# Splitting the gated outputs of an RWKV-7 layer in the rounds that make them, and loading the split halves at the output projection

## The chip, the cores and the metric

The kernel runs on one core of a Trainium2 chip. The metric is the device time of one execution in microseconds (us). Names of engines as in the profile: PE is TensorE (matmuls), PEld its weight loads, DVE is VectorE, ACT is ScalarE, POOL is GpSimd, SP is SyncE, which here only issues DMAs. A q behind a name (SPq) is the engine's instruction queue.

## The reference, cut to what matters

Two residual layers over 512 tokens of width 2048. Layer 0 is gated differential attention; the change is in layer 1, RWKV-7 time mixing:

```python
for i in range(DEPTH):                       # DEPTH = 2
    hn = rms_norm(x, norm_w[i])
    ...
    x = x + out

def rwkv7_mixer(h, ...):
    p = h @ w_in                             # r, k, v, gate g and two low-rank parts
    p = p + (token_shift(p) - p) * mu
    ...
    y = wkv7_scan(rh, decay, kh, vh, -kk, kk * ah)   # 32 heads of 64, a state of 64x64 per head
    ...                                      # group norm over each head, bonus term
    y = y.reshape(B, T, RW_WIDTH) * jax.nn.silu(g)   # the gated output, 512 x 2048
    return y @ w_out, v_first                # the output projection, 2048 x 2048
```

## The kernel before

**Split products.** Every large product of float32 matrices is made of three fp32r matmuls: each operand is split into a high part (hi, a copy rounded to fp32r) and a low part (lo, operand minus hi), and hi·hi, hi·lo and lo·hi are added up in PSUM. `split_w` splits a weight block: it is loaded to `wraw` (512 KB, SP issues the load at L78), ACT copies the high part to `wh` (L105), DVE subtracts the low part to `wl` (L106). The tokens that weights are multiplied with stand in two pools of 16 places each, `hH` and `hL`, one place per 128 channels ("row" k: 128 x 512).

**Layer 1** runs in 16 rounds j, one pair of heads (128 channels) each. `proj(i, j)` projects the layer's tokens to r, k, v or gate (48 matmuls, L125). The scan of the pair before is cut into steps that a `Chain` puts between those matmuls: matmuls `sm` (L1654, L1665, L1672) and `Y` on PE, copies `rhs` and `VS` on ACT (L1657, L1667), `VS` on DVE (L1676), `SA` and `Sg` on POOL (L1660, L1663). Each round solves a small triangular system `Tm` on DVE (L1516, L1518, behind POOL's memset at L1507); it goes to DRAM (`td`, L1526), comes back in four small loads `TT<-td` on SP (L1545), and DVE transposes it (`T`, L1555) for 32 small matmuls `px` (L1561), from which the next scan starts. The output of a pair is group-normed and multiplied by its gate (`mixv`, made by `shift_mix` on ACT at L1283 and DVE at L1284, weighted at L1620). `gated` does the last product on DVE (L1627) and has POOL store the row to `yd2` in DRAM (L1628).

**Output projection.** When the tokens of the layer are no longer used (during the projections of the last two gates), `split_rows` loads the rows of 14 pairs from `yd2`, in the order 8 to 13, then 0 to 7, to work tiles `yr` (SP, L462), and splits each to a place of `hH` (ACT, L452) and `hL` (DVE, L453). The last two rows are split straight from SBUF later. `seven_early` then computes output columns 0 to 1023. It begins with plain products of rows 8 to 13 and the first weight blocks, which `loader` fetches to three buffers `wraw`, while the last pair's scan still runs between them; then come seven Strassen products ("11", "12", "S1" and so on), whose summed rows (`frow`, L687, L699, L700) are formed from `yd2` as well. `between(n)` puts the end of the last two pairs between these pieces. `seven` computes columns 1024 to 2047. `acc` (L1875) are the residual's blocks.

The Tile scheduler sets the order of each engine's instructions and DMA issues by program order and priority (`high_priority(offset)` moves instructions ahead; `AHEAD` is 2000); every engine works its row off in order, and so does each queue. Tiles of one tag share buffers, so a load to a tag waits for the last reader of the buffer.

Of the kernel before, what the change touches and what calls it, by code (L numbers as in the profile page):

```python
# [13 lines left out]
F32 = mybir.dt.float32  # L14
F32R = mybir.dt.float32r
# [8 lines left out]
P = 128  # L24
D = 2048
T = 512
# [12 lines left out]
AHEAD, SCAN, SOLVE = 2000, 3000, 4000  # L39
# [34 lines left out]
def load_w(g, raw, part, k0, ks, queue=None):  # L74

    w, c = part
    with g.tc.issue_after(g.last) if g.last and not queue else ExitStack():
        ld = (queue or g.nc.sync).dma_start(out=raw[:, ks.start : ks.stop], in_=w[c][:, k0 + ks.start : k0 + ks.stop])  # L78
    g.last = ld.ins if g.last and not queue else g.last
    return ld.ins  # L80
# [367 lines left out]
def split_row(g, yr):  # L448
    nc = g.nc
    hh = g.hp.tile([P, T], F32R, name="hH", tag="hH")  # L450
    hl = g.hp.tile([P, T], F32R, name="hL", tag="hL")
    nc.scalar.copy(hh[:], yr)  # L452
    g.rowsplit = nc.vector.tensor_sub(hl[:], yr, hh[:].bitcast(F32)).ins  # L453
    return hh, hl


def split_rows(g, src, tags, bufs, order):

    out = {}
    for i, k in enumerate(order):  # L460
        yr = g.work.tile([P, T], F32, name="yr", tag=tags[i % len(tags)], bufs=bufs)
        g.nc.sync.dma_start(out=yr[:], in_=src[k * P : (k + 1) * P, :])  # L462
        out[k] = split_row(g, yr[:])
    return [out[k] for k in sorted(out)]


NH4 = 8
KG = 2
# [417 lines left out]
    done("21")  # L886


def loader(g, w, homes):

    homes = list(homes)

    def load(k0, c):
        homes.append(homes.pop(0))
        pool, tag, bufs = homes[-1]
        raw = pool.tile([P, KG, 512], F32, name="wraw", tag=tag, bufs=bufs)
        g.fetched = load_w(g, raw, (w, c), k0, slice(0, KG))
        return raw

    return load  # L900


def flat(t):

    n = "abc"[: len(t.shape) - 1]
    n = " ".join(n)
    return t[:].rearrange(f"p {n} -> p ({n})").rearrange("p (k c) -> p k c", k=KG)


def layer0(g, aps):  # L910
    nc, tc = g.nc, g.tc
    with ExitStack() as cx:
# [197 lines left out]
        def banks(i):  # L1110
            if i < 2:
                return [g.pp.tile([P, 512], F32, name="pp", tag="pp") for _ in range(2)]
            return [g.ps.tile([P, 512], F32, name="z", tag="pa", bufs=2) for _ in range(2)]

        T2 = g.work.tile([P, KG, 512], F32, name="T2", tag="Tb", bufs=1)
        load = loader(g, aps["da_w_out"], ((g.wraw, "wraw", 3), (g.work, "V", 1), (g.wraw, "wraw", 3),
                                              (g.work, "G", 1), (g.wraw, "wraw", 3)))

# [420 lines left out]
def t_combine(g, j, p, lead):  # L1539

    nc, w, TT = g.nc, g.work, g.TT[j % 2]
    for h in range(2):
        for half in range(2):
# [3 lines left out]
                in_=g.td[j % 2].rearrange("q (g l) t -> (q g) l t", g=NG)[:, l0 : l0 + NC_, :]).ins  # L1547
    T1 = w.tile([P, NC_, HALF], F32, name="T1", tag="T1", bufs=1)
    X = w.tile([P, NC_, HALF], F32, name="X", tag="X", bufs=1)
    px = g.ps.tile([P, 512], F32, name="px", tag="pd", bufs=1)  # L1550
    yield lead
    for h in range(2):
        r_ = slice(h * C, h * C + C)
        with g.tc.issue_after(g.centred) if g.centred else ExitStack():
            nc.vector.transpose(T1[r_], TT[r_, :, h, 0:HALF])  # L1555
    yield GAP_T
    N = NC_ * HALF
    blocks = [(h, h * C, slice(h * C, h * C + HALF), slice(h * C + HALF, h * C + C)) for h in range(2)]
    for c in range(NC_):
        for h, b0, lo, hi in blocks:  # L1560
            nc.tensor.matmul(px[hi, c * HALF : (c + 1) * HALF], p.G[lo, c, 0, h, HALF:C], T1[lo, c, :],  # L1561
                             start=True, stop=True, tile_position=(b0, b0 + HALF))
# [49 lines left out]
def gate(g, j, gps, tag="v", later=None):  # L1612
    nc, w = g.nc, g.work
    gt = shift_mix(g, gps, P, *mus(g, 3, j), tag, 1)
    th = w.tile([P, T], F32, name="thg", tag="thg", bufs=1)
    nc.scalar.activation(th[:], gt[:], AF.Tanh, scale=0.5)

    def weighted():
        with g.tc.issue_after(g.solved) if later else ExitStack():
            nc.vector.scalar_tensor_tensor(gt[:], th[:], 1.0, gt[:], ALU.add, ALU.mult)  # L1620
        return gt

    return weighted if later else weighted()


def gated(g, j, p, gt):
    g.nc.vector.tensor_mul(gt[:], gt[:], p.y[:])  # L1627
    g.nc.gpsimd.dma_start(out=g.yd2[j * P : (j + 1) * P, :], in_=gt[:])  # L1628


HEADS = ((0, slice(0, C)), (1, slice(C, P)))
# [106 lines left out]
def layer1(g, aps):  # L1738
    nc, tc = g.nc, g.tc
    with ExitStack() as cx:  # L1740
# [3 lines left out]
        w = g.work  # L1744
        pairs = []

        def proj(i, j, **k):
            return unit_chan(g, (aps["rw_w_in"], i * KT + j), P, **k)[0]
# [9 lines left out]
        def receptances(j):  # L1758
            return shift_mix(g, proj(0, j), P, *mus(g, 0, j), "r", 1)
# [6 lines left out]
        def weigh():  # L1766
            for i, weighted in weights:
                gated(g, i, pairs[i], weighted())
            weights.clear()

        begin(0)
        r = receptances(0)
        for j in range(D // P):
# [44 lines left out]
            if j + 1 < D // P:  # L1818
                r = receptances(j + 1)
            weigh()  # L1820
            if j == LAG:
                gated(g, 0, pairs[0], first)
# [3 lines left out]
        gts = [gate(g, j - 1, gps)]  # L1826

        gts.append(gate(g, j, proj(3, j), "E"))
        rows = split_rows(g, g.yd2, ("r", "k", "th0", "th1", "l", "f", "xH", "xL"), 1, [*range(8, j - 1), *range(8)])

        halves = [0, 2, 8, 10], [4, 6, 12, 14]
        sums = []
        one = lambda *tags: [(w, t, {"BKT": 2, "VS": 2, "y": 4}.get(t, 1)) for t in tags]
        homes = ({"S1": one("BKT"), "S2": one("VS"), "S4": one("l", "f"), "S3": one("y", "y")},
                 {"S1": one("th0", "th1"), "S2": one("r", "k"), "S4": one("xH", "xL"), "S3": one("g0", "k2")},
                 {"S1": one("BKT"), "S2": one("VS"), "S4": one("E", "thg"), "S3": one("yc", "v")},
                 {"S1": one("X", "T1", "Tm", "n2"), "S2": one("y", "y"), "S4": one("n0"), "S3": one("n1")})

# [31 lines left out]
        def residual(c0, nm, tag, bufs, after):  # L1870
            t, c = PLACES[nm]
            a = w.tile([P, 2, 512], F32, name="acc", tag=tag, bufs=bufs)
            c0 += c * 512
            with tc.issue_after(after):
                nc.sync.dma_start(out=a[:], in_=g.xd[t * 256 : t * 256 + 256, c0 : c0 + 512].rearrange("(t p) c -> p t c", p=P))  # L1875
            return [a[:, i, :] for i in range(2)]

        def stores(c0, acc):
            def done(nm):
                t, c = PLACES[nm]  # L1880
                for i, a in enumerate(acc[nm]):
                    r0, c_ = (2 * t + i) * P, c0 + c * 512
                    nc.scalar.dma_start(out=aps["out"][r0 : r0 + P, c_ : c_ + 512], in_=a)
            return done

        def banks(i):
            if i == 0:
                return [g.pp.tile([P, 512], F32, name="pp", tag="pp") for _ in range(2)]
            return [g.ps.tile([P, 512], F32, name="pt", tag=("pb", "pc")[i - 1], bufs=2) for _ in range(2)]

        acc = {nm: residual(0, nm, *at, g.blocks) for nm, at in zip(("11", "21", "12", "22"), (("AR", 3), ("AR", 3), ("n0", 1), ("n1", 1)))}
        T1 = w.tile([P, KG, 512], F32, name="T1", tag="LT", bufs=1)
        load = loader(g, aps["rw_w_out"], [(g.wraw, "wraw", 3)])
        seven_early(g, aps["rw_w_out"], load, rows, sums, 0, 1, acc, [flat(g.TT[0]), T1], banks,
                    stores(0, acc), [h[:2] for h in halves], (8, 10, 12), 14, between)
        acc = {nm: residual(1024, nm, "AR", 3, g.loaded) for nm in ("11", "21", "22", "12")}
# [2 lines left out]
        load = loader(g, aps["rw_w_out"], [(w, "G1", 2) if i in (1, 4) else (g.wraw, "wraw", 3) for i in range(8)])  # L1899
# [3 lines left out]
@with_exitstack  # L1903
def body(ctx, tc, nc, aps):
    g = Ctx()
    g.nc, g.tc = nc, tc
    g.last, g.first, g.centred = None, [], None
    g.chains, g.later, g.state, g.copied = [], [], None, None
    g.const = ctx.enter_context(tc.tile_pool(name="const", bufs=1))
    g.small = ctx.enter_context(tc.tile_pool(name="small", bufs=2))  # L1910
    g.hp = ctx.enter_context(tc.tile_pool(name="hp", bufs=16))
    g.wraw = ctx.enter_context(tc.tile_pool(name="wrawp", bufs=3))
    g.wh = ctx.enter_context(tc.tile_pool(name="whp", bufs=2))
    g.wl = ctx.enter_context(tc.tile_pool(name="wlp", bufs=2))
    dr = ctx.enter_context(tc.tile_pool(name="dr", bufs=1, space=DRAM))
    g.ys = [dr.tile([D - 256, T], F32, name=f"ys{i}") for i in range(2)]
    g.yd2 = dr.tile([D, T], F32, name="yd2")
    g.xd = aps["x1"] if "x1" in aps else dr.tile([T, D], F32, name="xd")
    g.ltd = dr.tile([2, 2, 2, NC_, HALF + 1, HALF], F32, name="ltd")
    g.td = dr.tile([2, HALF // NG, P, HALF], F32, name="td")  # L1920
    g.ident = g.const.tile([P, P], F32, name="ident")
    g.fixed = g.const.tile([P, 16], F32, name="fixed")
    g.neglam, g.subw = g.fixed[:, 0:1], g.fixed[:, 1:3]
    make_identity(nc, g.ident)
    for n, layer in ((4, layer0), (2, layer1)):
        with tc.tile_pool(name="pp", bufs=n, space=PSUM) as g.pp, \
                tc.tile_pool(name="ps", bufs=1, space=PSUM) as g.ps:
            layer(g, aps)
# [42 lines left out]
```

## Time and profile before

| | |
|---|---|
| median of 3 runs (lowest to highest) | 2051.22 us (2050.8 to 2052.6) |
| profiled execution, its time | 2051.32 us |
| span of the profiled execution | 2049.6 us |
| granted TensorE clock | 1.00 |
| busy in 2049.6 us: PE, DVE, ACT, POOL | 2032.6, 1626.3, 1139.3, 409.4 us |
| layer 0 to about 1000 us: PE busy, DMA share | 995.30 us of 1000, 0.72 |
| rounds of layer 1, 1000 to 1865 us | PE 858.74 us of 865, DMA share 0.33 |
| output projection, 1865 us to the end | PE 178.56 us of 184.60, DMA share 0.78 |

The profiled execution is one run of the program; its span lies 1.7 us under the time of that run. Shares of busy time are averages over a stretch. A timeline row gives start and length in us, engine, line, operation, output<-input; in brackets stands how long the engine had been idle and which instruction's end it then waited for. Matmul rows overlap, as matmuls are pipelined: 0.39 us long each, but starting 0.23 us apart.

### The profile page before, as it was taken

Reading aid. Unit: us, or ns where it says so; the run is one execution under the profiler, and the core shown is the slowest. Engines: PE = TensorE matmul, PEld = TensorE weight load, DVE = VectorE, ACT = ScalarE, POOL = GpSimd, SP = SyncE. Lnnn points to the kernel's source line nnn. Section 1 sums busy time; section 2 is a strip of 40 time slices with the busy share of each in tenths; the row PEclk is TensorE's granted clock in tenths of the full one; section 3 lists DMA queues with packets and bytes.
Section 4 is the critical chain, followed back from the end, with each engine's and each line's share of the span. In section 5 each row is a group of like instructions: output and inputs, shape, how many; then the busy total and the mean of one; then the engine's idle time right before and its main releaser. Section 6 shows DMA issues by size and latency. Waiting matters only on the chain. (4 is left out here: it accounts for less than half of the span.)

```text
span 2049.6 us, 34167 instructions
## 1 busy us (share of the span) xinstructions
PE 2032.6 (99%) x11898; PEld 1668.7 (81%) x11898; DVE 1626.3 (79%) x4126; ACT 1139.3 (56%) x2264; POOL 409.4 (20%) x786
## 2 busy tenths in 40 slices
PE   9999999999999999999999999999999999999999
PEld 8888888888888888888877788888888888877787
DVE  7988988888898977575787888877778878778865
ACT  5765656565666544355565555555555555546433
POOL 1020111102011000121122322222232222232211
PEclk9999999999999999999999999999999999999999
DMA  8487978879787965723323323233333332346796
GB/s 288 156 165 193 180 173 184 165 193 165 190 180 171 270 218 176 174 93 108 103 79 92 93 82 96 83 101 98 98 98 88 95 88 88 101 137 217 178 270 142
DMA packets 160845, 300.90 MB, mean 147 GB/s; under 512 B 64560, under 2 KB 81968, under 8 KB 160672
## 3 DMA queue, kind: packets, MB, share of 16 engines
q1 hardware_dynamic: 110416, 183.34, 28.4%
q0 software_dynamic: 26528, 92.98, 23.9%
q10 hardware_dynamic: 23728, 22.40, 3.4%
q8 instruction: 94, 1.54, 0.3%
q14 instruction: 79, 0.65, 0.1%
HBM read 274.48 MB, written 24.18 MB: 146 GB/s over the span
## 5 line engine op out<-in xcount | busy, mean ns | idle before, releaser
L106 DVE TENSOR_TENSOR wl<-wraw,wh 128x1024 fp32r<-128x1024 f32 (+1 forms) x284 | 347.5, 1224 | 155.2 <-ACT wh L105 146.1
L105 ACT CAST wh<-wraw 128x1024 fp32r<-128x1024 f32 (+1 forms) x284 | 297.4, 1047 | 232.2 <-PE pp L125 102.8
L125 PE MATMUL pp<-hL,wh 128*128 128x512 f32 x1024 | 413.5, 404 | 0.0
L125 PE MATMUL pp<-hH,wl 128*128 128x512 f32 x1024 | 413.1, 403 | 0.0
L125 PE MATMUL pp<-hH,wh 128*128 128x512 f32 x1024 | 412.3, 403 | 0.1
L125 PEld LDWEIGHTS pp<-hH,wh 128*128 128x128 f32 x1024 | 193.1, 189 | 34.5 <-ACT wh L105 0.4
L125 PEld LDWEIGHTS pp<-hL,wh 128*128 128x128 f32 x1024 | 193.1, 189 | 33.6
L125 PEld LDWEIGHTS pp<-hH,wl 128*128 128x128 f32 x1024 | 193.2, 189 | 32.5
L572 PE MATMUL pp<-wh,hH 128*128 128x512 f32 x448 | 176.8, 395 | 0.0
L572 PE MATMUL pp<-wh,hL 128*128 128x512 f32 x448 | 175.8, 393 | 0.0
L1516 DVE SCALAR_TENSOR_TENSOR tmpl<-LT,Tm 128x60 f32<-128x60 f32 (+24 forms) x496 | 135.0, 272 | 13.3
L1660 POOL COPY SA<-VS 64x64 f32<-64x64 f32 x224 | 59.4, 265 | 405.4 <-DVE VS L1676 367.4
L572 PE MATMUL pp<-wl,hH 128*128 128x512 f32 x448 | 140.2, 392 | 0.0
L125 PE MATMUL pp<-wl,hH 128*128 128x512 f32 x340 | 133.7, 393 | 0.0
L125 PE MATMUL pp<-wh,hH 128*128 128x512 f32 x340 | 133.3, 392 | 0.1
L125 PE MATMUL pp<-wh,hL 128*128 128x512 f32 x340 | 133.0, 391 | 0.1
L1518 DVE TENSOR_TENSOR Tm<-Tm,tmpl 128x60 f32<-128x60 f32 (+24 forms) x496 | 103.6, 209 | 11.7
L1657 ACT COPY rhs<-sm 64x64 f32<-64x64 f32 x256 | 53.1, 207 | 83.7 <-PE sm L1654 80.7
L572 PEld LDWEIGHTS pp<-wl,hH 128*128 128x128 f32 x448 | 84.4, 188 | 17.3
L572 PEld LDWEIGHTS pp<-wh,hH 128*128 128x128 f32 x448 | 84.2, 188 | 17.5 <-issue 0.4
L572 PEld LDWEIGHTS pp<-wh,hL 128*128 128x128 f32 x448 | 84.2, 188 | 16.0
L1667 ACT COPY VS<-sm 64x64 f32<-64x64 f32 x256 | 52.9, 206 | 75.2 <-PE sm L1665 69.2
(433 smaller groups left out, 4438.4 us busy)
## 6 DMA issues: line engine op xcount, KB each, us to landing
wraw<-in_rw_w_in_dram SPq DMA_DIRECT2D x128, 512.0 KB
wraw<-in_da_w_in_dram SPq DMA_DIRECT2D x75, 512.0 KB
wraw<-in_da_w_in_dram POOLq DMA_DIRECT2D x28, 512.0 KB, 6.6
wraw<-in_da_w_out_dram SPq DMA_DIRECT2D x26, 512.0 KB
Ta<-in_da_w_in_dram POOLq DMA_DIRECT2D x21, 512.0 KB, 5.5
Tb<-in_da_w_in_dram POOLq DMA_DIRECT2D x21, 512.0 KB, 5.7
Tc<-in_da_w_in_dram POOLq DMA_DIRECT2D x21, 512.0 KB, 5.3
Td<-in_da_w_in_dram POOLq DMA_DIRECT2D x21, 512.0 KB, 5.6
```

Of the source, the lines that this page charges most:

```text
L105: a = nc.scalar.copy(hi[:, ks], raw[:, ks])
L106: d = nc.vector.tensor_sub(lo[:, ks], raw[:, ks], hi[:, ks].bitcast(F32))
L125: m = nc.tensor.matmul(out, a, b, start=s, stop=e, skip_group_check=skip)
L572: m = nc.tensor.matmul(out[t][:], x, wt[lo][:, k, :], start=first, stop=end and lo == 1 and k == KG - 1, skip_group_check=True)
L1516: nc.vector.scalar_tensor_tensor(tt, LT[:, i : i + 1, i + 1 :].to_broadcast([P, s, n]), n2[:, i : i + 1], Tm[:, 0:s, i : i + 1].to_broadca ...
L1518: nc.vector.tensor_add(Tm[:, 0:s, i + 1 :], Tm[:, 0:s, i + 1 :], tt)
L1657: nc.scalar.copy(rhs[r_, :], sm[r_, h * C : h * C + C])
L1660: nc.gpsimd.tensor_copy(p.SA[r_, c - 1, :], VS[r_, c, h, :])
L1667: g.copied = nc.scalar.copy(VS[r_, c, h, :], sm[r_, P : P + C])
```

## The change

In rounds 0 to 13 `gated` also splits the row (ACT copy to `n0`, DVE subtract to `n1`) and POOL stores both halves to two DRAM tensors `ys`, which layer 0 had used for the same purpose. `load_split` takes the place of `split_rows`: it loads both halves straight to the tokens' places, two loads of 256 KB per row, rows 8 to 13 at the old place and rows 0 to 7 behind the residual's blocks. The loads of the first `loader` get the priority `AHEAD`. The store to `yd2` stays, since the summed rows are formed from it. Lines of the kernel after are 1 to 7 higher than those before from L897 on.

```diff
-def split_rows(g, src, tags, bufs, order):
+def load_split(g, order):
     out = {}
-    for i, k in enumerate(order):
-        yr = g.work.tile([P, T], F32, name="yr", tag=tags[i % len(tags)], bufs=bufs)
-        g.nc.sync.dma_start(out=yr[:], in_=src[k * P : (k + 1) * P, :])
-        out[k] = split_row(g, yr[:])
-    return [out[k] for k in sorted(out)]
+    for k in order:
+        out[k] = [g.hp.tile([P, T], F32R, name=n, tag=n) for n in ("hH", "hL")]
+        for x, d in zip(out[k], g.ys):
+            g.rowsplit = g.nc.sync.dma_start(out=x[:].bitcast(F32), in_=d[k * P : (k + 1) * P, :]).ins
+    return list(out.values())
...
-def loader(g, w, homes):
+def loader(g, w, homes, offset=0):
...
-        g.fetched = load_w(g, raw, (w, c), k0, slice(0, KG))
+        with g.tc.high_priority(offset=offset):
+            g.fetched = load_w(g, raw, (w, c), k0, slice(0, KG))
...
 def gated(g, j, p, gt):
     g.nc.vector.tensor_mul(gt[:], gt[:], p.y[:])
     g.nc.gpsimd.dma_start(out=g.yd2[j * P : (j + 1) * P, :], in_=gt[:])
+    if j < D // P - 2:
+        hi, lo = [g.work.tile([P, T], F32R, name=n, tag=n, bufs=1) for n in ("n0", "n1")]
+        g.nc.scalar.copy(hi[:], gt[:])
+        g.nc.vector.tensor_sub(lo[:], gt[:], hi[:].bitcast(F32))
+        for x, d in zip((hi, lo), g.ys):
+            g.nc.gpsimd.dma_start(out=d[j * P : (j + 1) * P, :], in_=x[:].bitcast(F32))
...
-        rows = split_rows(g, g.yd2, ("r", "k", "th0", "th1", "l", "f", "xH", "xL"), 1, [*range(8, j - 1), *range(8)])
+        rows = load_split(g, range(8, j - 1))
...
         acc = {nm: residual(0, nm, *at, g.blocks) for nm, at in ...}
+        rows[:0] = load_split(g, range(8))
         T1 = w.tile([P, KG, 512], F32, name="T1", tag="LT", bufs=1)
-        load = loader(g, aps["rw_w_out"], [(g.wraw, "wraw", 3)])
+        load = loader(g, aps["rw_w_out"], [(g.wraw, "wraw", 3)], AHEAD)
```

Three places show how the change moves instructions; in each, numbers behind a name tell buffers apart.

SP at the start of the output projection, before: `wraw_20539` and `wraw_20611` are the third and fourth block of the plain products, `acc` the residual.

```order
L1545 DMA TT1_9497<-td_80 32x8x32
L462 DMA yr_20321<-yd2_77 128x512
L462 DMA yr_20339<-yd2_77 128x512
L462 DMA yr_20345<-yd2_77 128x512
L462 DMA yr_20351<-yd2_77 128x512
L462 DMA yr_20357<-yd2_77 128x512
L462 DMA yr_20363<-yd2_77 128x512
L462 DMA yr_20369<-yd2_77 128x512
L1875 DMA acc_20375<-xd_78 128x2x512
...
L78 DMA wraw_20539<-in_rw_w_out_dram 128x1024
L78 DMA wraw_20611<-in_rw_w_out_dram 128x1024
```

The same place after, with `wraw_20595` and `wraw_20667` for the same two blocks:

```order
L463 DMA hH_20375<-ys0_75 128x512
L1546 DMA TT1_9497<-td_80 32x8x32
...
L78 DMA wraw_20595<-in_rw_w_out_dram 128x1024
L463 DMA hL_20376<-ys1_76 128x512
L78 DMA wraw_20667<-in_rw_w_out_dram 128x1024
L463 DMA hH_20379<-ys0_75 128x512
L463 DMA hL_20380<-ys1_76 128x512
L463 DMA hH_20383<-ys0_75 128x512
L463 DMA hL_20384<-ys1_76 128x512
L463 DMA hH_20387<-ys0_75 128x512
```

The two blocks moved ahead of the rows 9 to 13 and of the residual; the rows became two loads each.

DVE in the projection before last, before: the two transposes `T1_20171` and the first weight block's low part `wl_20391`.

```order
L1284 SCALAR_TENSOR_TENSOR mixv_20196<-pp_20043,mu_1989,mixv_20196 128x511
L1555 STREAM_TRANSPOSE T1_20171<-TT1_9497 64x256
L69 SCALAR_TENSOR_TENSOR rs_t_20183<-rs_t_20183,var_20178 128x8
L453 TENSOR_TENSOR hL_20312<-yr_20309,hH_20311 128x512
L71 SCALAR_TENSOR_TENSOR rs_i_20182<-rs_t_20183,rs_i_20182 128x8
L1620 SCALAR_TENSOR_TENSOR mixv_20196<-thg_20199,mixv_20196 128x512
L1555 STREAM_TRANSPOSE T1_20171<-TT1_9497 64x256
L106 TENSOR_TENSOR wl_20391<-wraw_20388,wh_20390 128x1024
```

After, the same two transposes and the same block (`wl_20447`):

```order
L687 TENSOR_TENSOR frow_20574<-frow_20574 128x2x256
L1285 SCALAR_TENSOR_TENSOR mixv_20280<-pp_20127,mu_1989,mixv_20280 128x511
L1556 STREAM_TRANSPOSE T1_20255<-TT1_9497 64x256
L69 SCALAR_TENSOR_TENSOR rs_t_20267<-rs_t_20267,var_20262 128x8
L700 TENSOR_TENSOR fS3_20583<-frow_20574,fS3_20582 128x512
L71 SCALAR_TENSOR_TENSOR rs_i_20266<-rs_t_20267,rs_i_20266 128x8
L106 TENSOR_TENSOR wl_20447<-wraw_20444,wh_20446 128x1024
L1556 STREAM_TRANSPOSE T1_20255<-TT1_9497 64x256
```

The row's split is gone, forms of the summed rows (L687, L700) stand in its place, and the weight's low part moved ahead of the second transpose.

DVE in the round where the first row (`mixg0`) is gated, before:

```order
L1627 TENSOR_TENSOR mixg0_10375<-mixg0_10375,y_9873 128x512
L1518 TENSOR_TENSOR Tm_10809<-Tm_10809,tmpl_10810 128x5x15
L1516 SCALAR_TENSOR_TENSOR tmpl_10810<-LT_10808,Tm_10809 128x70
L1518 TENSOR_TENSOR Tm_10809<-Tm_10809,tmpl_10810 128x5x14
L1516 SCALAR_TENSOR_TENSOR tmpl_10810<-LT_10808,Tm_10809 128x65
L1676 SCALAR_TENSOR_TENSOR VS_10493<-sm_11183,gam_9985,Sg_11190 64x64
```

And after:

```order
L1628 TENSOR_TENSOR mixg0_10375<-mixg0_10375,y_9873 128x512
L1519 TENSOR_TENSOR Tm_10809<-Tm_10809,tmpl_10810 128x5x15
L1517 SCALAR_TENSOR_TENSOR tmpl_10810<-LT_10808,Tm_10809 128x70
L1519 TENSOR_TENSOR Tm_10809<-Tm_10809,tmpl_10810 128x5x14
L1633 TENSOR_TENSOR n1_11310<-mixg0_10375,n0_11309 128x512
L1517 SCALAR_TENSOR_TENSOR tmpl_10810<-LT_10808,Tm_10809 128x65
L1683 SCALAR_TENSOR_TENSOR VS_10493<-sm_11183,gam_9985,Sg_11190 64x64
```

The subtract `n1` came in ahead of the scan's `VS`; the rest kept its order.

## The prediction

> **What bounds the kernel now.** I read the page first, then the waits of TensorE, then busy time by stretch, then the chain of waits where the second layer's output projection begins, and last the timelines of the engines at the places the change touches.
>
> From the page, then PE's waits over the whole run (total us, times, longest):
>
> ```profile
> PE 2032.6 (99%) x11898; PEld 1668.7 (81%) x11898; DVE 1626.3 (79%) x4126; ACT 1139.3 (56%) x2264; POOL 409.4 (20%) x786
> ```
>
> ```profile
> PE sm L1654 <- DVE VS L1676: 2.9, 6, 0.9
> PE sm L1665 <- ACT rhs L1657: 1.8, 3, 0.8
> ```
>
> PE is busy for 2032.6 of 2049.6 us, so 17.0 us is all that a change off PE could ever give, start and drain of the program included. The change touches no matmul. Three stretches (us, busy time of each engine, clock, DMA share, GB/s) show how little is left where it acts:
>
> ```profile
> 1500.00:1550.00 50.00, 49.96 (x382) 41.12 (x381) 37.88 (x104) 27.07 (x62) 15.09 (x35) 1.00 0.34 98
> 1850.00:1875.00 25.00, 25.00 (x221) 20.11 (x220) 23.34 (x66) 15.69 (x29) 2.20 (x4) 1.00 0.71 217
> 1875.00:1900.00 25.00, 23.98 (x119) 18.01 (x117) 21.78 (x39) 14.79 (x40) 9.52 (x19) 1.00 0.71 238
> 1900.00:1925.00 25.00, 24.81 (x165) 19.62 (x164) 21.93 (x45) 10.40 (x19) 6.35 (x9) 1.00 0.69 186
> ```
>
> A round in mid-scan has 0.04 us of PE idle in 50. Over the 75 us where rows were split and weights fetched, PE is idle for 0 + 1.02 + 0.19 = 1.21 us. DVE is nearly full there (23.34 of 25), but PE doesn't wait for it. The one visible stall is on this chain (start, length, what):
>
> ```profile
> 1873.45 10.25 DMA wraw<-in_rw_w_out_dram
> 1883.72 0.45 ACT wh L105
> ...
> 1884.68 0.62 ACT hH L452
> ```
>
> The third block to go through the weight buffers is issued at 1873.45 and lands 10.25 us later behind other loads; ACT, in order, then does the weight's copy and a row's copy before the scan's rhs. On PE's timeline the sm matmul behind that rhs stands so:
>
> ```profile
> 1884.42 0.39 PE L125 MATMUL pt<-wh,hL 128*128 128x512 f32 x1
> 1884.65 0.40 PE L125 MATMUL pt<-wh,hH 128*128 128x512 f32 x1
> 1885.80 0.43 PE L1665 MATMUL sm<-rhs,TT 128*128 128x64 f32 x2 [0.74 <-ACT rhs L1657]
> ```
>
> Matmuls start 0.23 us apart; here it takes 1.15, so 0.92 of the 1.21 is lost at this one place.
>
> **The change part by part.** The span is 2049.6 us, the profiled execution 2051.32, 0.10 above the median 2051.22. I sum against the execution and take the 0.10 off.
>
> *What leaves the end.* Fourteen rows are no longer loaded as one tile and split there:
>
> ```profile
> L462 SPq DMA_DIRECT2D yr<-yd x14: 319/327/423, 1787.2 to 1871.1; - x14
> L452 ACT CAST hH<-yr x14: 603/616/624, 1861.0 to 1877.6; 128x512 fp32r<-128x512 f32 x14
> L453 DVE TENSOR_TENSOR hL<-yr,hH x14: 675/684/693, 1862.6 to 1878.3; 128x512 fp32r<-128x512 f32 x14
> ```
>
> That is 14 x 0.616 = 8.6 us of ACT and 14 x 0.684 = 9.6 us of DVE gone from 1861 to 1879. PE waited for almost none of it. What it does free is the 0.92 at 1885.80, and most of the other 0.29 of idle time, where PE or its operands stand behind row splits on ACT and DVE. I take -1.2: the block's load now stands ahead of the rows and the residual loads on SP, and no row copy stands before the scan's rhs. The ends are -1.5 (the records' ends are modelled, so a gap may be a little longer than the idle time shown) and -0.3 (if the block still lands too late for its place).
>
> *What enters each round.* Rounds 0 to 13 get an ACT copy (0.62), a DVE subtract (0.68) and two more stores of 256 KB that POOL issues:
>
> ```profile
> L1628 POOL DMA_DIRECT2D yd<-mixv x14: 582/627/627, 1157.0 to 1882.9; - x14
> ```
>
> ```profile
> DMA to landing us min/median/max: 2.4/4.0/5.1
> ```
>
> So +1.25 us of POOL, and 0.5 MB, per round. A round at 1390 (ACT, DVE, POOL, PE timelines):
>
> ```profile
> 1390.01 0.44 ACT L1667 COPY VS<-sm 64x64 f32<-64x64 f32 x2
> 1394.96 0.63 ACT L1720 ACTIVATE ysq<-yc 128x512 f32<-128x512 f32 x1 [4.50 <-DVE yc L1711]
> ```
>
> ```profile
> 1390.13 1.21 DVE L106 TENSOR_TENSOR wl<-wraw,wh 128x1024 fp32r<-128x1024 f32 x1
> 1393.30 0.76 DVE L1709 TENSOR_REDUCE s<-Y 128x4 f32<-128x256 f32 x2 [1.96 <-PE Y L1698]
> ...
> 1395.83 0.44 DVE L1555 STREAM_TRANSPOSE T<-TT 64x256 f32<-64x256 f32 x1 [0.56 <-DMA TT<-td]
> ```
>
> ```profile
> 1391.52 0.31 POOL L1507 MEMSET Tm<- 128x256 f32 x1
> ```
>
> ```profile
> 1400.53 0.69 PE L1561 MATMUL px<-T,G 32*32 32x32 f32 x32
> ```
>
> ACT is idle for 4.50 us and DVE for 1.96 us just where the copy and the subtract stand, so both are hidden. The stores come out behind yd's; POOL's memset of Tm waits behind them for the subtract and 1.25 us of issues, about 2 us, and Tm is wanted in the next round's solve. The stores compete with the small TT loads, for which a transpose already waits 0.56. That transpose ends at 1396.27 and px starts at 1400.53, so 4.2 us of cover stands against at most about 2 us (two stores at the rate of the busiest stretch, below, are 1.3). Cost: 0 in the rounds from 1250 on (ends 0 and 0.5). Two early rounds lack the cover. First:
>
> ```profile
> 1084.78 0.27 DVE L1676 SCALAR_TENSOR_TENSOR VS<-sm,gam,Sg 64x64 f32<-64x64 f32 x1
> ```
>
> ```profile
> 1085.65 0.46 PE L1654 MATMUL sm<-VS,G 128*128 128x128 f32 x2 [0.87 <-DVE VS L1676]
> ```
>
> PE already waits 0.87 for VS there, and the subtract now stands ahead of it, with one instruction between: 0.68 less what DVE idles, so +0.6 (ends 0 and 0.7). Second, at 1222:
>
> ```profile
> 1220.90 0.44 DVE L1555 STREAM_TRANSPOSE T<-TT 64x256 f32<-64x256 f32 x1 [1.72 <-DMA TT<-td]
> ```
>
> ```profile
> 1223.64 0.69 PE L1561 MATMUL px<-T,G 32*32 32x32 f32 x30 [0.88 <-DVE T L1555]
> ```
>
> The transpose waits for TT and PE for the transpose, with no cover. Two stores are in the air shortly before: +0.4 (ends 0, if they have drained, and 1.3, both in full).
>
> *The extra stores and POOL's other work.* POOL's Sg has this row:
>
> ```profile
> L1663 POOL TENSOR_SCALAR Sg<-SA,gam x96: 439/447/1357, 1016.0 to 1901.1; 128x64 f32<-128x64 f32 x96
> ```
>
> Most take 0.447 us and some 1.357, three times as long. The Trainium skill, page "SBUF — State Buffer", section "SBUF: two separate sides", has VectorE and GpSimd share a port pair as an exclusive lock, which a VectorE operation with two SBUF inputs holds against a GpSimd one that reads SBUF; the subtract has two such inputs, which speaks against this change. The long Sg agree with a lock. By the row, the scan's waits for VS are 2.9 us in all, six of them, so I add nothing beyond the 0.6 at 1084; by the rule alone, 14 subtracts of 0.68 could hold up 9.5 us of POOL work.
>
> *The last projection.* DVE, PE and ACT:
>
> ```profile
> 1865.52 0.75 DVE L1284 SCALAR_TENSOR_TENSOR mixv<-pp,mu,mixv 128x511 f32<-128x511 f32 x1 [0.83 <-ACT mixv L1283]
> ...
> 1867.98 0.44 DVE L1555 STREAM_TRANSPOSE T<-TT 64x256 f32<-64x256 f32 x1
> ```
>
> ```profile
> 1869.21 0.69 PE L1561 MATMUL px<-T,G 32*32 32x32 f32 x32
> ```
>
> ```profile
> 1864.80 0.69 ACT L1283 ACTIVATE mixv<-pp,omu 128x512 f32<-128x512 f32 x1 [1.20 <-DMA yd<-mixv]
> ```
>
> Cover before px is 1869.21 - 1868.42 = 0.8 us. The first weight block's low part (1.2 us) moves ahead of the second transpose, and sums' forms of 0.68 each ahead of mixv in place of three hL subtracts of 0.68. ACT's mixv waits for the store of yd, now joined by two others. 1.2 more before the transpose, less 0.8 cover, is +0.4; a landing later by one store adds 0.1: +0.5 (ends 0 and 1.5).
>
> *Loads of split rows, and weights.* SP issued 7 rows in one go, one of them waiting for a tag:
>
> ```profile
> 1864.97 6.42 SPq L462 DMA_DIRECT2D yr<-yd x7
> ```
>
> Now 28 loads of 256 KB go out, 14 x 0.327 = 4.6 us more issue on SP, which is otherwise idle there, and 3.7 MB more bytes. From the block of weights at SP's fifth place after TT to row 13's low part it is 3 blocks and 12 loads, 4.7 MB, needed by about 1888, so from 1866 at 213 GB/s; on to row 7's low part 8.3 MB more, needed by about 1919, 245 GB/s over both. The rows of the stretches say what the queues can do: 217 GB/s at a share of 0.71 is 306 at full, 238 at 0.71 is 335. In slices of 0.75 us from 1875 to 1905:
>
> ```profile
> GB/s 322 369 270 268 254 363 415 421 415 429 415 306 355 153 98 27 186 300 224 164 333 186 93 169 355 98 0 76 300 311 22 0 147 300 246 5 0 0 0 0
> ```
>
> 415 to 429 is reached, and mostly under 300 is used after 1885. So the rows arrive in time, by 20% at the tightest: 0 (ends 0 and 3). An exception is row 9, wanted three matmuls into the first block's use and behind a weight block (the second one of token row 8) that waits for the first block's split; I have it landing at about 1874 for a use at 1873.2 to 1874.6: +0.2 (ends 0 and 1.5).
>
> *Forms moved later.* The second set of sums' forms now stands between the weights' splits of the first Strassen products:
>
> ```profile
> 1912.63 1.22 DVE L106 TENSOR_TENSOR wl<-T,wh 128x1024 fp32r<-128x1024 f32 x1
> ```
>
> This low part ended at 1913.85 in time for its first matmul a few tenths later; with one form of 0.68 more ahead of it, it ends at about 1914.5: +0.5 (ends 0 and 1).
>
> *Sum:* -1.2 + 0.6 + 0.4 + 0.5 + 0.2 + 0.5 = +1.0, and zero in the rounds and the later rows. 2051.32 + 1.0 = 2052.3 for an execution like the profiled one, 2052.2 for the median. All poor ends together: -0.3 + 0.5 + 0.7 + 1.3 + 1.5 + 3 + 1.5 + 1 = +9.2; all good ends: -1.5.
>
> **The rivals.** A measurement of this kernel can tell about 0.2%, 4.1 us, from no change, so faster means under 2047.1 and slower over 2055.3.
>
> *Only the gain.* Every added piece finds cover, and the stalls at the output projection go: -1.5, 2049.7. For it: DVE and ACT lose 18 us of work where DVE is fullest. Against it: the two early places are already waits.
>
> *Row loads starve PE (slower).* At the output projection, the rows stand behind weight loads on one queue that wait for buffers, and 13 MB goes through 53 us. For it: a share of 0.71 already and the 10.25 us landing above. Against it: rates up to 429 GB/s. It decides once the mean falls under 245 GB/s: at 220, 13 MB takes 59 us, 6 more, 2058. The Trainium skill, page "DMA: Bandwidth & Descriptors", section "Issuing engines are not separate DMA queues", says transfers started by SP, ACT and POOL interleave on the same 16 engines; the landing of 10.25 us, with seven rows and four residual blocks ahead of it, agrees.
>
> *The rounds pay (slower).* The subtract, the stores or POOL's issues hold up the scan by about the 0.6 of round 1084 in twelve more rounds: 1.0 + 7.2 = +8.2, 2060.4. For it: POOL's long Sg. Against it: 4.50 and 1.96 us idle in the quoted round, 4.2 us of cover before px. It decides if a round's POOL queue loses more than this cover.
>
> *Faster.* A gain over 4.1 us would need 2.7 times the 1.5 that I find; no row shows where it would come from.
>
> **How the numbers follow.** The forecast, +1.0 with some terms larger or smaller and still under +4.1: 0.65. Only the gain: 0.15. Row loads starve PE: 0.11. The rounds pay: 0.06. Faster by over 4.1 for a reason I don't see: 0.03. So faster 0.03, same 0.80, slower 0.17. The time is 2052.2. The range starts at 2049.4, a little under all good ends, and ends at 2056.5, into the case of late rows, leaving out its worse half and the rounds' case, about 0.15.
>
> **What the profile after would show.** PE's waits near 1885 lose the row for rhs, and the third weight block is issued near 1865 with a short landing: right on the first term. A wait for VS near 1084 of about 1.5 us, one of px near 1222 over 0.9 and a new one near 1869 for the transpose: right on the second to fourth. No PE wait for a row's hH or hL beyond 1.5 us, and busy PE of 50.0 in rounds: the covers hold. The prediction is wrong if PE waits for hH or hL between 1880 and 1920, if a round takes over 0.3 us longer, or if PE's idle time of 17.0 us falls by over 2.

## The result, and the profile after

The changed kernel takes 2061.68 us (median of 6 runs, 2058.43 to 2067.37) against 2051.01 us for the kernel before (6 runs, 2049.68 to 2052.6). The ratio is 1.0054 (95% interval 1.0039 to 1.0069): slower by 0.5%, outside the predicted range. Its profiled execution was the quickest of its six, 2058.43 us with a span of 2056.7, 7.1 us more than the span before.

From the page after, and PE's waits over the run (total us, times, longest):

```profile
PE 2035.4 (99%) x11898; PEld 1672.1 (81%) x11898; DVE 1625.4 (79%) x4126; ACT 1139.5 (55%) x2264; POOL 421.3 (20%) x814
```

```profile
PE px L1562 <- DVE T L1556: 3.8, 2, 2.0
PE gp L1458 <- DVE AR L1431: 3.1, 4, 1.0
PE sm L1661 <- DVE VS L1683: 2.6, 5, 0.9
PE sm L1672 <- ACT rhs L1664: 1.1, 1, 1.1
```

ACT and DVE do what they did: what left the end entered the rounds. In total the waits for VS and rhs did not grow. Two are new or larger: px for the transposes T, 3.8 us at two places, and `gp<-AR`, 3.1 us at four places, of which PE's waits of before show nothing. (`gp` are the matmuls that follow px; `AR`, the receptance weighted with the decay, is made on DVE.) Stretches of the kernel after:

```profile
1200.00:1250.00 50.00, 48.01 (x367) 39.79 (x366) 35.75 (x96) 25.87 (x60) 15.22 (x37) 0.97 0.36 104
1250.00:1800.00 550.00, 546.86 (x3914) 452.72 (x3913) 440.14 (x1217) 310.92 (x709) 158.21 (x367) 1.00 0.34 101
1875.00:1900.00 25.00, 23.19 (x160) 17.60 (x160) 14.49 (x29) 11.76 (x30) 4.79 (x12) 0.93 0.89 307
1900.00:1925.00 25.00, 25.00 (x172) 20.39 (x171) 17.90 (x34) 11.03 (x26) 5.00 (x13) 1.00 0.95 308
```

From 1250 to 1800 PE idled 0.04 us before (549.96 of 550 busy) and idles 3.14 now. And the granted clock, 1.00 in every stretch before, is 0.97 and 0.93 in two of them. Both hold a long wait for a transpose (PE's timeline, then three stretches around the first, and the two at half clock):

```profile
1224.97 0.69 PE L1562 MATMUL px<-T,G 32*32 32x32 f32 x30 [2.00 <-DVE T L1556]
...
1877.16 0.69 PE L1562 MATMUL px<-T,G 32*32 32x32 f32 x30 [1.79 <-DVE T L1556]
```

```profile
1225.00:1227.00 2.00, 2.00 (x51) 1.76 (x53) 2.00 (x4) 1.07 (x4) 1.20 (x2) 0.85 0.69 244
1227.00:1229.00 2.00, 2.00 (x22) 2.00 (x20) 1.83 (x8) 1.62 (x3) 0.37 (x1) 0.50 0.01 2
1229.00:1231.00 2.00, 2.00 (x40) 1.59 (x39) 1.62 (x7) 1.62 (x4) 0.48 (x1) 0.80 0.11 22
1226.40:1229.81 3.41, 3.41 (x50) 3.19 (x48) 3.10 (x13) 2.43 (x6) 0.96 (x1) 0.50 0.10 36
1878.34:1881.75 3.41, 3.41 (x9) 2.29 (x7) 2.71 (x8) 2.70 (x7) 0.11 (x1) 0.50 0.89 273
```

The clock column stands third from the end. From 1227 to 1229 it is 0.50: 22 matmuls in two us where 51 and 40 stand in the rows beside. The last two rows are the two stretches at half clock in full: 3.41 us each, so 1.7 us of lost clock each, 3.4 together. "PE busy" counts them as busy, so it could rise by 2.8 us with no matmul added.

How one round loses time (DVE, then PE):

```profile
1519.21 0.44 DVE L1556 STREAM_TRANSPOSE T<-TT 64x256 f32<-64x256 f32 x1 [2.17 <-DMA TT<-td]
...
1521.53 1.23 DVE L106 TENSOR_TENSOR wl<-wraw,wh 128x1024 fp32r<-128x1024 f32 x1
1522.67 0.74 DVE L1285 SCALAR_TENSOR_TENSOR mixr<-pp,mu,mixr 128x511 f32<-128x511 f32 x1
...
1523.60 0.68 DVE L1431 TENSOR_TENSOR AR<-mixr,E 128x512 f32<-128x512 f32 x1
```

```profile
1522.30 0.69 PE L1562 MATMUL px<-T,G 32*32 32x32 f32 x32
...
1524.33 2.06 PE L1458 MATMUL gp<-AR,BK 64*128 64x128 f32 x32 [0.99 <-DVE AR L1431]
```

The transpose waits 2.17 us for its TT load and ends 2.65 us ahead of px, so px itself loses nothing. But DVE works in order: behind the transpose stand the group norm's small steps, a weight's low part, mixr and AR. In the same round before, the transpose had waited 1.36 us, and AR was barely in time:

```profile
1518.87 0.69 DVE L1430 TENSOR_TENSOR AR<-mixr,E 128x512 f32<-128x512 f32 x1
```

```profile
1519.62 1.61 PE L1457 MATMUL gp<-AR,BK 64*128 64x128 f32 x24
```

In this round gp idled for 0.04 us behind AR. That is all of PE's idle time from 1250 to 1800 before, and the 0.04 in the row 1500 to 1550 of the prediction: the limit already showed there.

What grew is the time that the TT loads are under way, not the solve ahead of them: in this round the four loads are issued from 9.5 us ahead of px on, before (1509.05) as after (1512.86), with 2.0 us from the first issue to the last issue's end in both. In the other nine rounds to 1840 the last of them is issued at most 0.4 us later against px than before.

At the end, ACT's mixv waits for the landing of yd's store, and the second transpose now stands behind the weight's low part (ACT, then DVE):

```profile
1872.71 0.69 ACT L1284 ACTIVATE mixv<-pp,omu 128x512 f32<-128x512 f32 x1 [4.61 <-DMA yd<-mixv]
```

```profile
1875.40 1.23 DVE L106 TENSOR_TENSOR wl<-wraw,wh 128x1024 fp32r<-128x1024 f32 x1 [0.16 <-ACT wh L105]
1876.66 0.44 DVE L1556 STREAM_TRANSPOSE T<-TT 64x256 f32<-64x256 f32 x1
```

The 7.1 us, by the shift of the px matmuls' start against the same round before: +0.2 up to 1222 (1222.51 to 1222.73), +2.6 more by 1285 (1282.60 to 1285.45), +3.1 more from there to 1875 (1869.21 to 1875.12), and +1.2 from there to the end: 3.5 for the wait of px and the half clock, less 2.3 that was gained.

### The profile page after: what moved, and what is told of

It is laid out like the page before. It is cut to its first block, busy times and chain, and to the rows that moved or that the text cites. A ratio compares the mean times of both kernels' runs of the same rounds, so it can differ in the third digit from the quotient of the medians.

```text
span 2056.7 us, 34262 instructions
## 1 busy us (share of the span) xinstructions
PE 2035.4 (99%) x11898; PEld 1672.1 (81%) x11898; DVE 1625.4 (79%) x4126; ACT 1139.5 (55%) x2264; POOL 421.3 (20%) x814
## 4 chain that ended last, share of the span: by engine, by line
PE 81%; DVE 8%; issue 4%; DMA 3%; ACT 2%; POOL 0%; SPq 0%; ACTq 0%; POOLq 0%; DVEq 0%
PE pp L125 40%; PE pp L572 24%; PE pt L125 2%; DVE wl L106 2%; PE gp L1458 2%; PE sc L125 1%; PE o L125 1%; PE sm L1661 1%; DMA TT<-td 1%; DMA TT<-in_rw_w_out_dram 1%; PE sm L1679 1%; PE sm L1672 1%; ACT wh L105 1%; DVE tmpl L1517 1%; PE pt L297 1%
```

## The experiments

Theory S: the two extra stores delay the small TT loads, and DVE's in-order work behind the transposes reaches PE late. Its rivals: D, the split's ACT and DVE work delays the scan; E, the loss is made at the output projection. The first four kernels were compared with 23 runs of the kernel before, median 2051.53.

**e1_rounds_only.** The changed kernel with `split_rows` and the `loader` of before: the rounds' part alone.

```diff
-        rows = load_split(g, range(8, j - 1))
+        rows = split_rows(g, g.yd2, (...), 1, [*range(8, j - 1), *range(8)])
-        rows[:0] = load_split(g, range(8))
-        load = loader(g, aps["rw_w_out"], [(g.wraw, "wraw", 3)], AHEAD)
+        load = loader(g, aps["rw_w_out"], [(g.wraw, "wraw", 3)])
```

> The kernel before with the rounds' part of the change alone: split and two more stores in rounds 0 to 13, output projection as before. Theory S (the stores delay the small TT loads, DVE stands in its transpose, and the work queued behind it, AR above all, reaches PE late): PE waits for the transposes near 1222 by 2.0 us and for AR in four rounds by 3.1 us, and a stretch at half clock after the 2.0 us wait: +5 to +9 us. Theory D (ACT copy and DVE subtract push the scan's work back): the same total, but without longer waits of the transposes for TT. Theory E (the loss is made at the output projection): within 1 us of before.

2062.95 us (6 runs, 2056.60 to 2068.34), ratio 1.0049 (1.0033 to 1.0065). The rounds' part alone costs as much as the whole change, though not all at the same places. PE's waits:

```profile
PE px L1562 <- DVE T L1556: 2.9, 3, 2.0
PE gp L1458 <- DVE AR L1431: 2.7, 4, 1.0
```

Behind the wait at 1225.95 the clock is 0.50 for 10.24 us, 5.1 us lost. With the old output projection PE also waits there, 1.5 us for mixE at 1886.62 and 1.6 for rhs at 1897.52, which the changed kernel does not.

**e2_end_only.** The other half.

```diff
 def gated(g, j, p, gt):
     ...
-    if j < D // P - 2:
-        hi, lo = ...                # and the copy, the subtract, both stores
```

> The changed kernel without the split and the stores in the rounds: the halves loaded at the output projection are those that layer 0 left in the same tensors, so the product is one of other numbers; loads, weights and order at the end as changed. Theories S and D: the rounds are as before, and at the end the weight's low part ahead of the second transpose costs a PE wait of 0 to 1.8 us, less 1.2 us of removed waits: -1 to +2 us. Theory E: +5 to +10 us.

2050.01 us (11 runs), ratio 0.9991 (0.9982 to 0.9999): 1.5 us less than before, with no wait for AR. Theory E falls. The loads of 28 half rows cost nothing where the stores are absent. From the first px of the last projection to the end this kernel takes 178.2 us, before 180.4: the end alone gains 2.2 us, near the 2.3 above. What the stores do to the end is not in this run.

**e3_split_only.** e1 without the two stores.

```diff
-        for x, d in zip((hi, lo), g.ys):
-            g.nc.gpsimd.dma_start(out=d[j * P : (j + 1) * P, :], in_=x[:].bitcast(F32))
```

> The kernel before with the ACT copy and the DVE subtract in rounds 0 to 13, but without the two stores, and with nothing reading the halves. Theory S: within 1 us of before. Theory D: +5 us or more, with the waits for AR. Theory E: within 1 us.

2051.87 us, ratio 1.0001 (0.9993 to 1.0010), no wait for AR. Theory D falls: ACT and DVE really have the room.

**e4_stores_only.** e1 with the stores, without the split.

```diff
-        hi, lo = ...
-        g.nc.scalar.copy(hi[:], gt[:])
-        g.nc.vector.tensor_sub(lo[:], gt[:], hi[:].bitcast(F32))
-        for x, d in zip((hi, lo), g.ys):
-            g.nc.gpsimd.dma_start(..., in_=x[:].bitcast(F32))
+        for d in g.ys:
+            g.nc.gpsimd.dma_start(out=d[j * P : (j + 1) * P, :], in_=gt[:])
```

> The kernel before with two more stores of the gated row (as it is, not split) in rounds 0 to 13, and nothing reading them: no ACT copy, no DVE subtract. Theory S: +4 to +9 us, with the transposes waiting longer for TT. Theory D and theory E: within 1 us of before.

2061.05 us, ratio 1.0047 (1.0035 to 1.0059). The stores alone make the loss:

```profile
PE gp L1458 <- DVE AR L1431: 3.7, 5, 1.7
PE px L1562 <- DVE T L1556: 2.2, 2, 2.0
```

PE also waits 0.9 us for mixE at 1882.95.

The next four went with 21 runs of before, median 2051.39.

**e6_stores_by_act.** e4 with `nc.scalar` in place of `nc.gpsimd` for the two stores.

> The kernel with the two stores alone (nothing split, nothing reading them), issued by ACT in place of POOL at the same place of the program. Theory S with all queues sharing the DMA engines: transposes wait for TT as with POOL's stores, +4 to +10 us. Theory P (it is POOL's queue: its way of issuing, or what stands behind the stores on POOL): 0 to +2 us.

2067.30 us, ratio 1.0074 (1.0060 to 1.0088).

```profile
PE gp L1458 <- DVE AR L1431: 6.5, 5, 1.9
```

It isn't POOL's queue, nor what stands behind the stores on POOL: issued elsewhere, the same stores cost more, 15.9 us by the medians, over the forecast of 10 at most. The Trainium skill, page "DMA: Bandwidth & Descriptors", section "Issuing engines are not separate DMA queues", says that such transfers interleave on the same 16 engines whoever starts them; this run agrees. (The landing of 10.25 us that the prediction set beside this rule does not bear on it: SP had issued all the loads named there.) Why ACT's are the worse is open. From 1250 to 1840 ACT issues both stores ahead of the first TT load of their round (10.3 and 9.9 us before px in most rounds, the load 9.6 to 9.1), POOL in e4 the second one only among them (8.7 to 7.7 us before px).

**e7_one_store.** e4 with `g.ys[:1]`, one extra store per round.

> The kernel with one store more per round in place of two (POOL, nothing split). Theory S: the transposes end about half as much later as with two, which is within the cover of most rounds: 0 to +4 us, with px near 1222 waiting 1.2 to 1.7 us and one or two waits for AR. A cost in proportion to the bytes: +4 to +5 us, half of that with two stores.

Median 2055.00, ratio 1.0013 (1.0004 to 1.0021). That is 3.6 us against 9.5 with two stores by the medians, 0.13% against 0.47% by the ratios. Half of e4's cost would be a ratio of 1.0018 to 1.0030, which touches this interval, so the time alone doesn't exclude a cost in proportion to the bytes. The waits show the cover: AR is waited for 0.7 us in all where e4 has 3.7, while px near 1222, with hardly any cover, waits 1.8 where e4 has 2.0. (The forecast for px was 1.2 to 1.7.)

**e8_late_transpose.** No store; a reduction on DVE between the transposes, in rounds 3 to 14.

```diff
+            if h and LAG < j < D // P - 1:
+                s = w.tile([P, 8], F32, name="late", tag="n0", bufs=1)
+                with g.tc.issue_after(first), g.tc.high_priority(offset=2 * SOLVE):
+                    nc.vector.reduce_sum(s[:, :8], p.AR[...]...to_broadcast([P, 8, T]), axis=AX.X)
+            first = nc.vector.transpose(T1[r_], TT[r_, :, h, 0:HALF]).ins
```

> The kernel before with no store added, but one long reduction of 4.3 us on DVE between the two transposes of rounds 3 to 14; it ends before px needs the transposes in most rounds. Theory S (what is queued on DVE behind the transposes is what makes PE wait): PE waits for AR by 0.3 to 1.3 us in most of the 12 rounds, +4 to +12 us, although not a byte more is moved and px waits for 0.9 us at most in rounds after 1250. Theory V (bytes or POOL): within 1 us of before.

A miss: 2132.24 us, ratio 1.0391 (1.0376 to 1.0405), far over both theories. The scheduler had changed the order: behind the second transpose AR now has only mixr and a weight's low part ahead of it, and px was moved in PE's order. PE then waited for other things:

```profile
PE sm L1659 <- POOL G L1573: 15.9, 11, 2.4
PE px L1566 <- DVE T L1560: 10.0, 13, 1.1
```

It is a different program and tells nothing of the chain through AR. What does tell it: in the rounds from 1250 to 1840 of the two kernels and of all experiments but e8 (11 kernels, 110 rounds), the lead of the second transpose's end over px can be set against the time that gp starts late, both from the timelines.

| transpose ends ahead of px by | rounds | gp late, lowest to highest |
|---|---|---|
| 3.6 us or more | 78 | 0.00 |
| 3.4 to 3.6 | 11 | 0.00 to 0.16 |
| 3.2 to 3.4 | 5 | 0.21 to 0.36 |
| 2.9 to 3.2 | 7 | 0.41 to 0.98 |
| 2.4 to 2.9 | 5 | 1.06 to 1.08 |
| under 2.4 | 4 | 1.65 to 2.02 |

Before, the ten rounds lead by 3.45 to 4.8 us; with both stores issued beside the TT loads 4 to 6 of ten fall under 3.4, without them or with later ones none. The lateness follows the lead, whatever kernel the round is in, with one addition: in three of the 110 rounds (1285 and 1760 of the changed kernel, 1405 of e6) AR itself took 1.07 to 1.11 us in place of 0.68 to 0.70. In just these three, POOL's copy of G had begun 0.04 to 0.08 us ahead of it. So about 0.4 us of each of the two 0.91 us waits in the changed kernel is AR's own length.

**e5_stores_late.** The changed kernel with a round's stores moved behind the copies of G that follow px.

```diff
+        store_halves(g, g.nc.gpsimd)          # what is still held, ahead of the new halves
...
-        for x, d in zip((hi, lo), g.ys):
-            g.nc.gpsimd.dma_start(...)
+        g.held = [(j, hi, lo)]
...                                            # in t_combine
-        copy(p.G[r_, :, 0, h, :], p.AR[r_, :, 0, :])
+        copied = copy(p.G[r_, :, 0, h, :], p.AR[r_, :, 0, :])
+    with g.tc.issue_after(copied.ins):
+        store_halves(g, nc.gpsimd if LAG < j < D // P - 1 else nc.scalar)
```

> The changed kernel with the two stores of a round issued later: behind the copies of G that follow px (on POOL; in the first and the last such round on ACT), so that the small TT loads and the transposes are done by then. Theory S (the stores delay the TT loads and DVE's in-order work behind the transposes): no wait for AR in the rounds, 0.9 us or less for px near 1222, clock 1.00; -2.5 to +1 us against before, near the -1.5 of the end alone. Theory V (the stores cost by their bytes or by POOL's issue time, wherever they stand): +4 to +10 us as in the changed kernel.

Half a miss: 2055.05 us, ratio 1.0018 (1.0010 to 1.0027). In the rounds theory S holds: no wait for AR, with the same stores. (px near 1222 still waits 1.36 us, over the 0.9 forecast, and the clock stays 1.00 there.) So theory V falls, but the total missed the forecast of +1 us at most. What the forecast missed went at the end: from the first px to the end 181.8 us, where e2 takes 178.2 (PE's timeline):

```profile
1872.08 0.69 PE L1562 MATMUL px<-T,G 32*32 32x32 f32 x30 [0.77 <-DVE T L1556]
...
1877.51 0.50 PE L125 MATMUL pp<-wh,hH 128*128 128x512 f32 x1 [1.17 <-DMA hH<-ys]
...
1879.17 0.50 PE L125 MATMUL pp<-wh,hL 128*128 128x512 f32 x1 [0.93 <-DMA hL<-ys]
```

Row loads stand on SP behind the fourth weight block, which waits for the first block's low part on DVE, and this one now stands ahead of the transpose.

**e9_mended.** e5 with these two orders turned round.

```diff
-        rows = load_split(g, range(8, j - 1))
+        with tc.high_priority(offset=AHEAD):
+            rows = load_split(g, range(8, j - 1))
...                                            # in t_combine
-            nc.vector.transpose(T1[r_], TT[r_, :, h, 0:HALF])
+            g.turned = nc.vector.transpose(T1[r_], TT[r_, :, h, 0:HALF]).ins
...                                            # in seven_early
-            plain(k0, c, (y, 0, s, e), (z, 256, s, e))
+            with g.tc.issue_after(g.turned) if s and c == c1 else ExitStack():
+                plain(k0, c, (y, 0, s, e), (z, 256, s, e))
```

> The changed kernel with three edits: the two stores of a round behind the copies of G as in e5_stores_late; the loads of rows 8 to 13 with the weights' priority, so that no row waits on SP behind the fourth weight block; and the first weight block's low part behind the second transpose on DVE. Theory S, with the losses of e5 at the end (0.96 us for px, 1.2 and 0.9 for row 9) put down to these two orders: no wait of PE for hH or hL, less than 0.8 us for px at the end, -2 to +0.5 us against before. If the losses of e5 have another cause: +2.5 to +4.5 us as there.

2050.66 us (11 runs) against 2051.39 (21), ratio 0.9996 (0.9987 to 1.0005). PE waits for no row and 0.67 us for px at the end; the rounds are full again:

```profile
1250.00:1800.00 550.00, 550.00 (x3928) 455.01 (x3927) 443.21 (x1222) 313.58 (x713) 157.17 (x369) 1.00 0.35 102
```

With the stores late and the two orders turned round the loss is gone; what each of the two orders is worth was not measured apart. A gain over the kernel before isn't shown: the interval holds 1.

**e10_weights_first.** The kernel before with the loader's priority alone.

```diff
-        load = loader(g, aps["rw_w_out"], [(g.wraw, "wraw", 3)])
+        load = loader(g, aps["rw_w_out"], [(g.wraw, "wraw", 3)], AHEAD)
```

> The kernel before with the loader's priority alone (weight loads of the first half earlier on SP; rows loaded and split as before). If the 0.9 us stall at 1885 comes from the third block's late issue: it is gone and the time is 0.5 to 1.5 us less than before. If it comes from ACT's row copies: no change, within 0.5 us.

It went with the 21 runs of e9. Median 2053.23, ratio 1.0006 (0.9997 to 1.0015): no gain. The stall at 1885 is gone, so it did come from the late block, but the 0.5 to 1.5 us that this was to give did not come: while the rows are still split on ACT and DVE there are others in its place (PE, 1780 to the end):

```profile
PE sm L1666 <- ACT rhs L1658: 2.0, 3, 1.4
PE pt L125 <- DVE wl L106: 0.7, 1, 0.7
PE pt L125 <- ACT wh L105: 0.7, 1, 0.7
```

## Why the prediction was wrong

**The step that failed** is the cost of the two stores in the rounds, "0 in the rounds from 1250 on (ends 0 and 0.5)". It set 4.2 us of cover before px against a transpose up to 2 us later. The delay was within its bound: over the ten rounds from 1250 to 1840 the mean lead fell from 4.33 to 3.60 us, and by 1.4 at most. The cover was the wrong one. px is not the first that waits: for AR, queued behind the transpose, the lead must be some 3.5 us by the table, and the thinnest round before had 3.45. I named what waits for the transpose, not what is queued behind it on DVE, and read the cover from one round. Four rounds lost 3.1 us (e4, e5, e6 and the table). The prediction's own sign, a round over 0.3 us longer, came in three of them.

**The second miss** is a term that is not in the sum: a stretch at half clock behind a long pause of PE, twice, 3.4 us in all. So the 7.1 us between the spans are 3.1 for AR, 2.9 for longer waits of px (1.1 and 1.8) and 3.4 for the clock, less 2.3 gained; the forecast had 0, 0.9 and nothing, less 1.2.

**The round at 1222**: forecast +0.4, at most 1.3. The wait grew by 1.1, within the ends; the half clock behind it took 1.7 us more.

**The last projection**: forecast +0.5, at most 1.5. Measured 1.8 of wait and 1.7 of half clock. The two mechanisms named, the weight's low part ahead of the transpose and the later landing of yd's store, were the ones. They added up instead of being partly covered: mixv came 2.0 us later than the round's shift.

**Right**: the removed stall (no wait for rhs after 1780, as forecast; the end gained 2.3 us in the changed kernel and 2.2 in e2, more than this term's -1.2 and its end of -1.5); the split's ACT and DVE work, hidden (e3); rows 10 to 13 and 0 to 7 in time (PE waits for no load of hH or hL in the changed kernel). The forecast +0.6 at 1084, +0.2 for row 9 and +0.5 for the forms did not come: PE's wait for VS stayed at 0.9, row 9 was in time, and no wait for wl appeared near 1915.

**The rivals**: "the rounds pay", given 0.06 and 2060.4, came nearest in size (its sum counts the 1.0 twice: 7.2 on 2052.2 is 2059.4). Of the three things it names, the stores were the one, but by another way: not the subtract nor POOL's issues, since e3 has the first and e6 takes the stores off POOL. The port rule that was weighed with it costs nothing that shows through the subtracts: e3, with all 14, lies between 1.4 us under and 2.1 us over before. The late rows did not occur in the changed kernel, and did in e5.

The changed kernel's median lies 3.3 us above its profiled execution. The six runs' mean clocks are 0.996 to 0.999, and the two at 0.996 are the slowest (2064.12 and 2067.37); a thousandth of the clock is 2 us. The same shows in e1: its two runs at clock 1.000 took 2056.60 and 2056.70 us, the four at 0.997 to 0.998 took 2062.52 to 2068.34. More or longer stretches at half clock in the slower runs are likely, but only the profiled run of each kernel has a trace.

## What to carry to other kernels

For an engine that waits, price the whole row behind it, not only the reader of its result: the cover is that of whichever queued instruction is wanted first. Small transfers that a chain waits for don't go well with bulk stores issued beside them; stores that nobody needs soon can wait until the small ones have landed. Read the granted clock by stretch beside the busy time: here a stall of 2.0 us on TensorE was followed by 1.7 us of lost clock that counts as busy.

## What the runs showed of the hardware

In these traces a pause of PE can bring on a stretch at half clock that is longer than itself, and the length of the pause alone does not decide. Without e8 it looks as if it did: of the eight pauses of 1.79 to 2.00 us of idle time seven have a clock of 0.50 from 0.3 us before their end to 1.7 us behind it, one (1.80 in e6, at 1527.55) has not, and no shorter one has. But in e8 ten of PE's waits for G are equally long, 1.34 to 1.37 us. At four of them the clock went to half within 0.7 us of their end, at six it did not, nor did it behind the pause of 2.74 us at 1943 (PE's timeline of e8, then a stretch behind each):

```profile
1298.84 0.38 PE L1659 MATMUL sm<-VS,G 128*128 128x128 f32 x1 [1.36 <-POOL G L1573]
1362.49 0.58 PE L1659 MATMUL sm<-VS,G 128*128 128x128 f32 x1 [1.35 <-POOL G L1573]
1943.37 0.50 PE L125 MATMUL pp<-wh,hH 128*128 128x512 f32 x1 [2.74 <-DVE mixv L1284]
```

```profile
1300.45:1303.86 3.41, 3.18 (x60) 2.70 (x60) 1.29 (x2) 2.15 (x5) 0.00 (x0) 1.00 0.00 0
1361.89:1368.71 6.82, 6.22 (x33) 4.92 (x35) 3.60 (x12) 2.31 (x6) 0.55 (x1) 0.50 0.24 77
1945.57:1952.40 6.83, 6.53 (x86) 4.59 (x85) 4.45 (x6) 6.01 (x14) 0.55 (x1) 1.00 0.61 217
```

What orders them better is a grid: in all 12 traces the stretches of constant clock are whole multiples of 3.41 us, but for the last one of the program (in the changed kernel 357, 1, 190, 1 and 51 of them). Cut by this grid, and up to 12 us from the end, the pieces at full clock in which PE idled 1.7 us or more by its records were all followed by half clock (9 of 9), of those with 1.3 to 1.7 us 5 of 16, of the others none. The pause of 2.74 us falls on two pieces, with 1.52 and 1.22 us of idle time. What decides between 1.3 and 1.7 us is open, and no kernel was made to vary a pause alone. In e1 the half clock lasted 10.24 us, three pieces.

The Trainium skill, page "TensorE: Matmul & The Clock Gate", section "Part 1: The HAM clock gate (the "warmup" mystery)", gives one idle window of about 3.4 us as what puts the array to half its clock. The traces agree on the half clock and on the 3.41 us, and differ on how idle such a window must be: 1.36 us of idle time in it was enough in e8, 1.65 in e6.
